# A hybrid decoder block on one core: new places in SBUF for the operands and weights of the split-precision matmuls

## The chip, the cores and the metric

The kernel runs on one core of one Trainium2 chip. The metric is the device time of one execution in microseconds, lower is better; the kernel before takes 1353.78 us (median of 3 runs, 1351.4 to 1355.38).

## The reference, cut to what matters

One layer of a decoder trunk is applied to a prompt of 256 tokens and to 8 sequences of 4 new tokens with state. All of it is float32; the model width is 2048.

```python
mod = silu(c) @ w_ada + b_ada                       # six parts of 2048: shift, scale, gate, twice
h = rmsnorm(x, norm1) * (1 + sc1) + sh1
proj = h @ w_in                                     # pooled channels, z, x/B/C, dt: 4632 columns
pool_out, new_pool = pool_mixer(u_pool, ...)        # windows 2, 4, 8, 16
ssd_out, new_conv, new_ssm = ssd_mixer(z, xbc, dt_raw, ...)   # conv, chunked scan, 24 heads
x = x + g1 * (concat(pool_out, ssd_out) @ w_out)
h2 = rmsnorm(x, norm2) * (1 + sc2) + sh2
up = h2 @ w_up                                      # gate and value, 2 x 5504 columns
x = x + g2 * ((silu(conv3(gate)) * val) @ w_down)
y = rmsnorm(x, norm_f)
```

The outputs are `y` for both kinds of token and the new pooling, convolution, scan and feed-forward states.

## The kernel before, in words

Features lie on the 128 partitions and the 288 tokens (256 + 32) along the free axis, so each of the four large projections (`w_in`, `w_out`, `w_up`, `w_down`) is a series of matmuls with a 128x128 block of weights as the stationary operand and a 128x288 block of activations streaming past it.

To keep float32 accuracy, both sides are split in two float32r parts, hi (the value rounded) and lo (what is left). `mm3` (lines 257 to 261) then issues three matmuls into one PSUM tile: weights hi x operand hi (line 259), weights hi x operand lo (line 260), weights lo x operand hi (line 261). Each of them loads its own stationary operand, so the hi weights are loaded twice. These triples are most of the kernel: k runs over the 16 blocks of the input width (15 or 14 for the three groups of the down projection), m over the output blocks.

Weights come in as one stream of 512 KB tiles of 1024 columns (`load`, line 229; issued by SyncE) into the buffers `raw`. ScalarE rounds a raw tile into the hi part and VectorE subtracts to give the lo part (`split`, lines 234 to 243) of a buffer `wsp`, 2112 columns (8448 bytes) per partition: hi at column 0, lo at column 1056. A wsp tile holds 8 blocks of weights, 512 bytes each. The class `_W` deals out buffers of `raw` and `wsp` in turn from the pools that are open: pool w1 (RAW1 raw and SPLIT1 split buffers) throughout, w0 (RAW0, SPLIT0) until the last of the six column groups of the input projection, w2 (RAW2, SPLIT2) from the sixth tile of the output projection on. With the values before that is 15 raw buffers, then 10, then 11.

The operand of a projection is 16 tiles `xop` (called h1k, mixk and h2k by stage; `new_operand`, line 194), each [128, 2, 288], 2304 bytes per partition: hi, then lo 1152 bytes on. The operand of the down projection is 17 rotating tiles `ahl` of the same form, made in `up_pair` (line 1143). The tag `xop` also holds the tiles `xf` of the final norm at the end.

`shift` (line 187) puts an unused gap in a pool so that what follows lies at a wanted place; the tuple PHASE gives its sizes in bytes for pools kp, ff, w2 and w0.

The order on the engines comes from a scheduler that keeps the program's priorities; `tc.high_priority` moves the splits ahead and `kpo` pins a few instructions in program order. Beside the projections TensorE runs the adaLN products (`ada_group_units`, `ada_part_units`; lines 339 and 380), which read raw tiles directly, the scan (`ssd_group`), the dt projection (lines 967 and 968, 64 columns of weights with hi and lo side by side in one wsp tile) and, during the gated MLP, the update of the sampled states (`state_units`, line 1181).

Of the kernel before, what the change touches and what calls it, by code (L numbers as in the profile page):

```python
# [11 lines left out]
F32 = mybir.dt.float32  # L12
F32R = mybir.dt.float32r
AF = mybir.ActivationFunctionType
ALU = mybir.AluOpType
PSUM = bass.MemoryType.PSUM

P = 128
D = 2048
KT = D // P  # L20
# [3 lines left out]
N = NP + NS  # L24
# [11 lines left out]
ET = XT + len(UEARLY) + 3 * ZEARLY  # L36
EPS = 1e-6
WU = (14, 2, 6)
RAW1, RAW2 = 10, 1
RAW0, SPLIT0 = 5, 1  # L40
SPLIT1, SPLIT2 = 2, 2
PHASE = (128, 32, 0, 128)
# [17 lines left out]
FK = 3  # L60
DGROUPS = [(0, 15), (15, 14), (29, 14)]
RAWC = 1024
CW = 3 + NP + NB * 7
CV = CW - 3

# [8 lines left out]
def _xbc_chunks(gi):  # L74
    k0, gk = KGROUPS[gi]
    mper = RAWC // (gk * P)
    return [(list(range(k0, k0 + gk)), list(range(m, min(m + mper, ET)))) for m in range(0, ET, mper)]
# [20 lines left out]
def _stream():  # L98
# [6 lines left out]
    for gi, (k0, gk) in enumerate(KGROUPS):  # L105
        per = RAWC // (256 * gk)
        for q in range(KT // per):
            s.add(("ada", gi, q), RAWC)
        if gi == len(KGROUPS) - 1:
# [5 lines left out]
    for part in (3, 4, 2, 5):  # L115
        for k in range(KT):
            for h in range(2):
                s.add(("adap", part, k, h), RAWC)
    for m in range(16):
# [16 lines left out]
def kernel(ctx: ExitStack, tc, ins, outs):  # L136
    nc = tc.nc
# [3 lines left out]
    kp = ctx.enter_context(tc.tile_pool(name="kp", bufs=1))  # L141
# [42 lines left out]
    xhi = [None]  # L184
    xlo = [None]
# [6 lines left out]
    shift(kp, PHASE[0], "x")  # L192

    def new_operand(name):
        pair = [kp.tile([P, 2, N], F32R, tag="xop", name=f"{name}k{k}", bufs=KT) for k in range(KT)]
        xhi[0] = [t[:, 0, :] for t in pair]
        xlo[0] = [t[:, 1, :] for t in pair]

    def col_sums(ps, src, rhs, first, last):

# [23 lines left out]
    wp = [None]  # L224

    def load(key):
        off, cols = S.items[key]
        t = wp[0].tile([P, RAWC], F32, tag="raw", name="raw_" + "_".join(map(str, key)))
        nc.sync.dma_start(t[:, :cols], wflat[off:off + P * cols].rearrange("(p n) -> p n", p=P))
        return t  # L230

    kpo = tc.keep_in_program_order

    def split(raw, a, n, name, eng=None, pin=False):
        pair = wp[0].tile([P, 2 * RAWC + 64], F32R, tag="wsp", name="wsp_" + name)
        hi, lo = pair[:, 0:RAWC], pair[:, RAWC + 32:2 * RAWC + 32]
        with tc.high_priority():
            i = nc.scalar.copy(hi[:, :n], raw[:, a:a + n])  # L238
            j = (eng or nc.vector).tensor_tensor(lo[:, :n], raw[:, a:a + n], hi[:, :n].bitcast(F32), ALU.subtract)  # L239
        if pin:  # L240
            kpo(i)
            kpo(j)
        return hi, lo

    def split_hi():
        pair = wp[0].tile([P, 2 * RAWC + 64], F32R, tag="wsp", name="wsp_xbc0_0")
        raw = load(("xbc", 0, 0))
        kpo(nc.scalar.copy(pair[:, 0:RAWC], raw))
        return pair, raw

    def split_xbc(gi, ci, pin=False):
        (ks, ms), key = _xbc_chunks(gi)[ci], ("xbc", gi, ci)
        return ready.pop(key, None) or split(load(key), 0, len(ms) * len(ks) * P, f"xbc{gi}_{ci}",
                                             nc.gpsimd if ci in PSPLIT.get(gi, ()) else None, pin)
# [8 lines left out]
    ready = {}  # L263
    first = []
# [134 lines left out]
    def samp(ap):  # L399
        return ap.rearrange("p (b l) -> p b l", b=NB)  # L400
# [20 lines left out]
    def normalize(k0, gk, r):  # L421
        xv = xav(k0, gk)
        kpo(nc.vector.tensor_tensor(xv, xv, r.unsqueeze(1).to_broadcast([P, gk, N]), ALU.mult))
# [58 lines left out]
    for q in range(4):  # L482
        t = mx.tile([P, 4, N], F32, tag="blk", name=f"xa{q}", bufs=4)
# [26 lines left out]

    cvp = [mx.tile([P, 5, CW], F32, tag="cvp", name=f"cvp{g}", bufs=4) for g in range(4)]

# [141 lines left out]
    def drain(gen):  # L654
        for _ in gen:
            pass
# [3 lines left out]
    def conv_group(g):  # L660
        cf = m2[0].tile([P, 5, CW], F32, tag="cf", name=f"cf{g}", bufs=2)
        cfs[g] = cf
# [46 lines left out]
    def ssd_group(g):  # L709
# [3 lines left out]
        def toks(r, c):  # L713

            return cff[:, r * CW + c * P:r * CW + c * P + P]

# [192 lines left out]
    shift(w0, PHASE[3], "v")  # L909
    wp[0].add(w0, RAW0, SPLIT0)  # L910
    modulate1(0, 1, "g0")
    pair, raw = first.pop()
    kpo(nc.vector.tensor_tensor(pair[:, RAWC + 32:2 * RAWC + 32], raw, pair[:, 0:RAWC].bitcast(F32), ALU.subtract))
    ready[("xbc", 0, 0)] = pair[:, 0:RAWC], pair[:, RAWC + 32:2 * RAWC + 32]
    ready[("xbc", 0, 1)] = split_xbc(0, 1, True)
    normalize(1, 3, rstd1)
    conv0 = conv_group(0)
# [35 lines left out]
    for gi in range(len(KGROUPS)):  # L953
        last = gi + 1 == len(KGROUPS)
        if last:
            wp[0].remove(w0)
            w0_ctx.close()
            m2[0] = mx_ctx.enter_context(tc.tile_pool(name="m2", bufs=1, reuse_waits="tile"))
            raw = load(("dt",))[:, 0:KT * 32].rearrange("p (k h) -> p k h", h=32)
            both = wp[0].tile([P, 2 * RAWC + 64], F32R, tag="wsp", name="wsp_dt")  # L960
            bv = both[:, 0:KT * 64].rearrange("p (k h) -> p k h", h=64)
            with tc.high_priority():
                nc.scalar.copy(bv[:, :, 0:32], raw)
                nc.vector.tensor_tensor(bv[:, :, 32:64], raw, bv[:, :, 0:32].bitcast(F32), ALU.subtract)
            ps = pm.tile([P, 512], F32, tag="mm", name="mm_dt")
            for k in range(KT):
                nc.tensor.matmul(ps[0:64, :N], bv[:, k, :], xhi[0][k], start=k == 0, stop=False)
                nc.tensor.matmul(ps[0:64, :N], bv[:, k, :], xlo[0][k], start=False, stop=k == KT - 1)
            dt_stage(ps)
        else:  # L970
            if gi == 3:
                nc.sync.dma_start(vec, ins["vec"])
            if gi == 4:
                late_loads()
            nxt = ada_group_units(gi + 1)
            k0, gk = KGROUPS[gi + 1]
        for i, m in enumerate(xbc_units(gi)):
            if not last:
                if gi == 0 and i in (4, 10, 16):
                    normalize(4 + 4 * ((i - 4) // 6), 4, rstd1)  # L980
                if i in VISIT[gi + 1][1]:
                    next(nxt)
                if i == ET - MOD[gi]:
                    drain(nxt)
                    modulate1(k0, gk, f"g{gi + 1}")
            else:
                pull(back, 0.5 if m < 20 else RB1) if m >= 9 else None
                pull(adas, RA1 / AY)
# [34 lines left out]
    for g in range(4):  # L1023
        for t in range(3):
            k = 4 + 3 * g + t
# [7 lines left out]
    ff = ctx.enter_context(tc.tile_pool(name="ff", bufs=1, reuse_waits="tile"))  # L1033
# [85 lines left out]
    def up_pair(j):  # L1119
        pg = up0[2 * j] if j < FK else project(("gate", j), KT)  # L1120
        gb = ff.tile([P, NG], F32, tag="gb", name=f"gb{j}", bufs=2)
        gs = gb[:, 2 + NP:].rearrange("p (b l) -> p b l", b=NB)
        nc.gpsimd.memset(gb[:, 0:2], 0.0)
        nc.gpsimd.tensor_copy(gs[:, :, 0:2], stf[:, j])
        nc.scalar.copy(gb[:, 2:2 + NP], pg[:, 0:NP])
        nc.scalar.copy(gs[:, :, 2:6], samp(pg[:, NP:N]))
        nc.gpsimd.tensor_copy(nff[:, j, 0:2], gb[:, NP:NP + 2])
        nc.gpsimd.tensor_copy(nff[:, j, 2:18].rearrange("p (b l) -> p b l", b=NB), gs[:, :, 4:6])
        fw = V_FW + 3 * j
        gc = ff.tile([P, NG], F32, tag="gc", name=f"gc{j}", bufs=2)  # L1130
        nv = NG - 2
        nc.vector.tensor_scalar(gc[:, :nv], gb[:, 0:nv], vec[:, fw:fw + 1], vec[:, V_FB + j:V_FB + j + 1],
                                ALU.mult, ALU.add)
        for i in (1, 2):
            nc.vector.scalar_tensor_tensor(out=gc[:, :nv], in0=gb[:, i:i + nv], scalar=vec[:, fw + i:fw + i + 1],
                                           in1=gc[:, :nv], op0=ALU.mult, op1=ALU.add)
        nc.scalar.activation(gc[:, :nv], gc[:, :nv], AF.Silu)
        pv = up0[2 * j + 1] if j < FK else project(("val", j), KT)
        act = ff.tile([P, N], F32, tag="act", name=f"act{j}", bufs=2)
        nc.vector.tensor_tensor(act[:, 0:NP], gc[:, 0:NP], pv[:, 0:NP], ALU.mult)  # L1140
        gcs = gc[:, 2 + NP:].rearrange("p (b l) -> p b l", b=NB)[:, :, 0:NL]
        nc.vector.tensor_tensor(samp(act[:, NP:N]), gcs, samp(pv[:, NP:N]), ALU.mult)
        ahl = ff.tile([P, 2, N], F32R, tag="ahl", name=f"ahl{j}", bufs=17)
        ah, al = ahl[:, 0, :], ahl[:, 1, :]
        nc.scalar.copy(ah, act)  # L1145
        nc.vector.tensor_tensor(al, act, ah.bitcast(F32), ALU.subtract)
        acts[j] = (ah, al)
# [232 lines left out]
```

## Time and profile before

| | |
|---|---|
| median of 3 runs | 1353.78 us |
| profiled execution, its own time | 1351.28 us |
| its span | 1349.3 us |
| TensorE busy | 1327.1 us (98%) |
| weight loads busy | 1242.1 us (92%) |
| VectorE, ScalarE, GpSimd busy | 819.4, 580.0, 229.0 us |
| granted TensorE clock | 0.997 mean |
| DMA, mean | 240 GB/s |

The profile is one execution. A group line reads: line of the kernel, engine, operation, tile written <- tiles read, shape, count | busy time in us, mean duration in ns | idle time of the engine before them and what ended it. Matmuls are pipelined, so their durations overlap and their ends are modelled: the distance from start to start is what counts. Where a line gives three durations, they are shortest/median/longest in ns, followed by the first and last start in us. A line that begins with two times joined by a colon is a stretch of the span, with the busy time and the count of each engine in it, the granted clock, the share of DMA time and GB/s.

### The profile page before, as it was taken

To read this page: it belongs to the slowest core of one execution; us is meant where nothing else is said; L and a number is where in the kernel's file an instruction comes from. 1 tells how busy PE (TensorE), PEld (TensorE's weight loads), DVE (VectorE), ACT (ScalarE), POOL (GpSimd) and SP (SyncE) were. 2 spreads that over 40 slices of the span, in tenths; PEclk is the share of its full clock that TensorE was granted. 3 is DMA by queue.
4 is the path that set the end of the run, shared out by engine and by line. 5 is a ranking of instruction groups with operands and counts; after the bars stand their busy time and mean duration, and the time that the engine had idled before them with its cause. 6 is when DMAs were issued, how large, how long until landed. Compare 5 with 4: busy or idle time off the path is not lost.

```text
span 1349.3 us, 26295 instructions
## 1 busy us (share of the span) xinstructions
PE 1327.1 (98%) x10541; PEld 1242.1 (92%) x10541; DVE 819.4 (61%) x1458; ACT 580.0 (43%) x934; POOL 229.0 (17%) x420
## 2 busy tenths in 40 slices
PE   9999999999999999999999999999999999999997
PEld 7889998777779889999999999999999999999997
DVE  5676669878664458655665445656655556666543
ACT  5333344578643335434343333444433334443442
POOL 0201001123222223110221001322210011122221
PEclk9999999999999999999999999999999999999998
DMA  9989779978789777777555565655555655665521
GB/s 379 407 335 360 285 271 336 355 263 333 301 328 368 286 248 253 248 300 246 184 185 184 163 181 184 206 182 198 181 173 165 189 194 188 198 194 187 186 84 70
DMA packets 97193, 323.25 MB, mean 240 GB/s; under 512 B 10736, under 2 KB 19760, under 8 KB 97072
## 3 DMA queue, kind: packets, MB, share of 16 engines
q1 hardware_dynamic: 93168, 310.70, 65.4%
q0 software_dynamic: 3184, 9.69, 1.9%
q8 instruction: 82, 1.34, 0.4%
q10 hardware_dynamic: 720, 1.19, 0.2%
q14 instruction: 39, 0.32, 0.1%
HBM read 309.84 MB, written 10.39 MB: 237 GB/s over the span
## 4 chain that ended last, share of the span: by engine, by line
PE 95%; DVE 2%; ACT 1%; issue 0%; DMA 0%; POOL 0%; DVEq 0%; POOLq 0%; ACTq 0%
PE mm_down L260 7%; PE mm_down L261 7%; PE mm_down L259 7%; PE mm_val L260 6%; PE mm_gate L260 6%; PE mm_gate L259 6%; PE mm_gate L261 6%; PE mm_val L261 6%; PE mm_val L259 6%; PE xbc L259 4%; PE xbc L260 4%; PE xbc L261 4%; PE adap L380 4%; PE mm_out L259 3%; PE mm_out L260 2%; PE mm_out L261 2%
## 5 line engine op out<-in xcount | busy, mean ns | idle before, releaser
L260 PE MATMUL mm_down<-ahl,wsp_down 128*128 128x288 f32 x688 | 204.3, 297 | 0.0
L261 PE MATMUL mm_down<-ahl,wsp_down 128*128 128x288 f32 x688 | 202.8, 295 | 0.0
L259 PE MATMUL mm_down<-ahl,wsp_down 128*128 128x288 f32 x688 | 202.1, 294 | 0.0
L260 PE MATMUL mm_val<-h2k,wsp_val 128*128 128x288 f32 x640 | 190.1, 297 | 0.0
L260 PE MATMUL mm_gate<-h2k,wsp_gate 128*128 128x288 f32 x640 | 190.0, 297 | 0.0
L261 PE MATMUL mm_gate<-h2k,wsp_gate 128*128 128x288 f32 x640 | 188.8, 295 | 0.0
L261 PE MATMUL mm_val<-h2k,wsp_val 128*128 128x288 f32 x640 | 188.8, 295 | 0.0
L259 PE MATMUL mm_gate<-h2k,wsp_gate 128*128 128x288 f32 x640 | 188.8, 295 | 0.0
L259 PE MATMUL mm_val<-h2k,wsp_val 128*128 128x288 f32 x640 | 188.0, 294 | 0.0
L239 DVE TENSOR_TENSOR wsp_down<-raw_down,wsp_down 128x1024 fp32r<-128x1024 f32 x96 | 107.3, 1118 | 121.9 <-ACT wsp_down L238 121.9
L239 DVE TENSOR_TENSOR wsp_gate<-raw_gate,wsp_gate 128x1024 fp32r<-128x1024 f32 x80 | 98.0, 1226 | 133.9 <-ACT wsp_gate L238 132.8
L238 ACT CAST wsp_down<-raw_down 128x1024 fp32r<-128x1024 f32 x96 | 92.2, 960 | 168.0 <-PE mm_down L261 118.2
L238 ACT CAST wsp_gate<-raw_gate 128x1024 fp32r<-128x1024 f32 x80 | 84.0, 1050 | 158.8 <-PE mm_gate L261 75.4
L238 ACT CAST wsp_val<-raw_val 128x1024 fp32r<-128x1024 f32 x80 | 84.1, 1051 | 127.9 <-issue 111.3
L259 PE MATMUL xbc<-h1k,wsp_xbc 128*128 128x288 f32 x448 | 132.5, 301 | 5.1 <-ACT h1k L444 3.1
L260 PE MATMUL xbc<-h1k,wsp_xbc 128*128 128x288 f32 x448 | 132.2, 298 | 0.5 <-DVE h1k L445 0.5
L259 PEld LDWEIGHTS mm_down<-ahl,wsp_down 128*128 128x128 f32 x688 | 129.6, 188 | 0.0
L260 PEld LDWEIGHTS mm_down<-ahl,wsp_down 128*128 128x128 f32 x688 | 129.3, 188 | 0.0
L261 PEld LDWEIGHTS mm_down<-ahl,wsp_down 128*128 128x128 f32 x688 | 129.2, 188 | 0.0
L261 PE MATMUL xbc<-h1k,wsp_xbc 128*128 128x288 f32 x448 | 128.8, 294 | 0.0
L259 PEld LDWEIGHTS mm_gate<-h2k,wsp_gate 128*128 128x128 f32 x640 | 120.5, 188 | 5.0 <-ACT ahl L1145 4.2
L259 PEld LDWEIGHTS mm_val<-h2k,wsp_val 128*128 128x128 f32 x640 | 120.6, 188 | 0.0
(320 smaller groups left out, 2979.5 us busy)
## 6 DMA issues: line engine op xcount, KB each, us to landing
raw_adap<-wflat SPq DMA_DIRECT2D x128, 512.0 KB, 6.7
raw_gate<-wflat SPq DMA_DIRECT2D x80, 512.0 KB, 3.6
raw_val<-wflat SPq DMA_DIRECT2D x80, 512.0 KB, 3.6
raw_ada<-wflat SPq DMA_DIRECT2D x64, 512.0 KB, 9.1
raw_xbc<-wflat SPq DMA_DIRECT2D x55, 512.0 KB, 9.5
raw_down<-wflat SPq DMA_DIRECT2D x48, 512.0 KB, 3.5
raw_out<-wflat SPq DMA_DIRECT2D x32, 512.0 KB, 6.0
raw_down<-wflat SPq DMA_DIRECT2D x32, 384.0 KB, 3.0
```

Of the source, the lines that this page charges most:

```text
L238: i = nc.scalar.copy(hi[:, :n], raw[:, a:a + n])
L239: j = (eng or nc.vector).tensor_tensor(lo[:, :n], raw[:, a:a + n], hi[:, :n].bitcast(F32), ALU.subtract)
L259: nc.tensor.matmul(ps, whi[:, w], bh, start=first, stop=False)
L260: nc.tensor.matmul(ps, whi[:, w], bl, start=False, stop=False)
L261: nc.tensor.matmul(ps, wlo[:, w], bh, start=False, stop=last)
L380: i = nc.tensor.matmul(ps[32 * j:32 * j + 32, :512], sc_c[:, k, :], raw[:, (j % 2) * 512:(j % 2) * 512 + 512], start=(k == ay - 1), stop=( ...
```

## The change

Five things move together. The operand tiles grow from 2304 to 2560 bytes; in them hi begins at byte 16 and lo at byte 1200, 1184 bytes on (4 x 256 + 160), where it was 1152 on. The split weights' tile keeps its size; in it hi begins at byte 16 and lo at byte 4208, 4192 bytes on (16 x 256 + 96), where it was 4224 on. The dt projection's tile begins at byte 16 as well. To make room for the larger tiles (16 xop and 17 ahl, 256 bytes each), RAW1 goes from 10 to 9 and RAW2 from 1 to 0, so there are 14, then 9, then 9 raw buffers. No instruction is added, removed or reordered in the code.

```diff
-RAW1, RAW2 = 10, 1
+RAW1, RAW2 = 9, 0
...
+OPC, WSC = 640, 2 * RAWC + 64
+OPH, OPL = 4, 300
+WH, WL = 4, 1052
...
     def new_operand(name):
-        pair = [kp.tile([P, 2, N], F32R, tag="xop", name=f"{name}k{k}", bufs=KT) for k in range(KT)]
-        xhi[0] = [t[:, 0, :] for t in pair]
-        xlo[0] = [t[:, 1, :] for t in pair]
+        pair = [kp.tile([P, OPC], F32R, tag="xop", name=f"{name}k{k}", bufs=KT) for k in range(KT)]
+        xhi[0] = [t[:, OPH:OPH + N] for t in pair]
+        xlo[0] = [t[:, OPL:OPL + N] for t in pair]
...
     def split(raw, a, n, name, eng=None, pin=False):
-        pair = wp[0].tile([P, 2 * RAWC + 64], F32R, tag="wsp", name="wsp_" + name)
-        hi, lo = pair[:, 0:RAWC], pair[:, RAWC + 32:2 * RAWC + 32]
+        pair = wp[0].tile([P, WSC], F32R, tag="wsp", name="wsp_" + name)
+        hi, lo = pair[:, WH:WH + RAWC], pair[:, WL:WL + RAWC]
...
-            both = wp[0].tile([P, 2 * RAWC + 64], F32R, tag="wsp", name="wsp_dt")
-            bv = both[:, 0:KT * 64].rearrange("p (k h) -> p k h", h=64)
+            both = wp[0].tile([P, WSC], F32R, tag="wsp", name="wsp_dt")
+            bv = both[:, WH:WH + KT * 64].rearrange("p (k h) -> p k h", h=64)
...
-        ahl = ff.tile([P, 2, N], F32R, tag="ahl", name=f"ahl{j}", bufs=17)
-        ah, al = ahl[:, 0, :], ahl[:, 1, :]
+        ahl = ff.tile([P, OPC], F32R, tag="ahl", name=f"ahl{j}", bufs=17)
+        ah, al = ahl[:, OPH:OPH + N], ahl[:, OPL:OPL + N]
```

`split_hi` and the first projection's first tile are rewritten in the same way, with hi and lo handed over as two pieces.

More of the change, by code (lines that the diff above doesn't have):

```diff
@@ L245, in split_hi @@
     def split_hi():
-        pair = wp[0].tile([P, 2 * RAWC + 64], F32R, tag="wsp", name="wsp_xbc0_0")
+        pair = wp[0].tile([P, WSC], F32R, tag="wsp", name="wsp_xbc0_0")
+        hi, lo = pair[:, WH:WH + RAWC], pair[:, WL:WL + RAWC]
         raw = load(("xbc", 0, 0))
-        kpo(nc.scalar.copy(pair[:, 0:RAWC], raw))
-        return pair, raw
+        kpo(nc.scalar.copy(hi, raw))
+        return hi, lo, raw
     def split_xbc(gi, ci, pin=False):
@@ L911 @@
     modulate1(0, 1, "g0")
-    pair, raw = first.pop()
-    kpo(nc.vector.tensor_tensor(pair[:, RAWC + 32:2 * RAWC + 32], raw, pair[:, 0:RAWC].bitcast(F32), ALU.subtract))
-    ready[("xbc", 0, 0)] = pair[:, 0:RAWC], pair[:, RAWC + 32:2 * RAWC + 32]
+    hi, lo, raw = first.pop()
+    kpo(nc.vector.tensor_tensor(lo, raw, hi.bitcast(F32), ALU.subtract))
+    ready[("xbc", 0, 0)] = hi, lo
     ready[("xbc", 0, 1)] = split_xbc(0, 1, True)
```

## Prediction

> **What bounds the kernel now.** I read the page's first part, the granted clock and the chain of waits first.
>
> ```profile
> span 1349.3 us, 26295 instructions
> PE 1327.1 (98%) x10541; PEld 1242.1 (92%) x10541; DVE 819.4 (61%) x1458; ACT 580.0 (43%) x934; POOL 229.0 (17%) x420
> PEclk9999999999999999999999999999999999999998
> PE 95%; DVE 2%; ACT 1%; issue 0%; DMA 0%; POOL 0%; DVEq 0%; POOLq 0%; ACTq 0%
> ```
>
> TensorE is the bound, at full clock, and 95% of the chain is its own work. No other engine can give back more than a few microseconds, so the change is worth what it does to the distance between matmuls. Next, the groups by shape, one line of the three in `mm3` (259 is hi weights x hi operand, 260 hi x lo, 261 lo x hi):
>
> ```profile
> L259 PE MATMUL mm_down<-ahl,wsp_down 128*128 128x288 f32 x688 | 202.1, 294 | 0.0
> L259 PE MATMUL mm_gate<-h2k,wsp_gate 128*128 128x288 f32 x640 | 188.8, 295 | 0.0
> L259 PE MATMUL mm_val<-h2k,wsp_val 128*128 128x288 f32 x640 | 188.0, 294 | 0.0
> L259 PE MATMUL xbc<-h1k,wsp_xbc 128*128 128x288 f32 x448 | 132.5, 301 | 5.1 <-ACT h1k L444 3.1 <-DVE ada L369 1.6 <-ACT cvp L649 0.2
> L259 PE MATMUL mm_out<-mixk,wsp_out 128*128 128x288 f32 x256 | 75.7, 296 | 0.0
> L259 PE MATMUL mm_uz<-h1k,wsp_uz 128*128 128x288 f32 x128 | 40.0, 313 | 0.0
> L259 PE MATMUL mm_up<-h2k,wsp_upk 128*128 128x288 f32 x96 | 27.7, 294 | 1.4 <-ACT h2k L417 1.4
> ```
>
> 688+640+640+448+256+128+96 = 2896 triples. One nanosecond per triple is 2.9 us of the kernel. Durations overlap, so I took the distance from counts and first and last starts, in two stretches that hold nothing but the down projection (720 to 800 us, then 1250 to 1330 us):
>
> ```profile
> L259 PE MATMUL mm_down<-ahl,wsp_down x204: 291/293/294, 720.0 to 799.8; 128*128 128x288 f32 x102
> L260 PE MATMUL mm_down<-ahl,wsp_down x205: 297/297/297, 719.7 to 800.0; 128*128 128x288 f32 x103
> L261 PE MATMUL mm_down<-ahl,wsp_down x204: 292/294/295, 719.9 to 799.7; 128*128 128x288 f32 x102
> L259 PE MATMUL mm_down<-ahl,wsp_down x201: 296/296/297, 1249.9 to 1329.9; 128*128 128x288 f32 x101
> L260 PE MATMUL mm_down<-ahl,wsp_down x201: 297/297/297, 1250.0 to 1330.0; 128*128 128x288 f32 x101
> L261 PE MATMUL mm_down<-ahl,wsp_down x201: 297/298/298, 1249.7 to 1329.7; 128*128 128x288 f32 x101
> ```
>
> Same code, same shape, same clock, two locked patterns. First: 203 steps in 79.8 us, a triple in 393.3 ns. Second: 200 steps in 80.0 us, 400.0 ns. The step between them is 6.7 ns. In the second pattern the three durations add to 891 for 400 ns, so a distance is a duration less 163.6: 297 is 133.4, 291 is 127.4. Line 260 stands at 133.4 in both; 259 and 261 are what differ. The patterns alternate:
>
> ```profile
> 640.00:1330.00 690.00, 690.00 (x5221) 690.00 (x5220) 395.88 (x573) 277.39 (x391) 124.77 (x247) 1.00 0.55 177
> 655.00:675.00 20.00, 20.00 (x155) 20.00 (x154) 11.07 (x15) 8.43 (x13) 2.45 (x6) 1.00 0.53 164
> 680.00:700.00 20.00, 20.00 (x152) 20.00 (x151) 11.70 (x17) 7.71 (x12) 5.73 (x9) 1.00 0.57 188
> 705.00:725.00 20.00, 20.00 (x155) 20.00 (x154) 11.68 (x18) 7.02 (x10) 3.98 (x8) 1.00 0.60 188
> 1290.00:1330.00 40.00, 40.00 (x303) 40.00 (x302) 18.85 (x28) 19.75 (x29) 9.05 (x14) 1.00 0.11 34
> ```
>
> 155 matmuls in 20 us, then 152, then 155 (columns: TensorE, weight loads, VectorE, ScalarE, GpSimd, clock, DMA share, GB/s). The slow pattern stays at a DMA share of 0.11 and at 0.57, so traffic is not its cause. What flips it is a pair of other matmuls put in between, the state update's, whose weights `bm` lie in two buffers 1152 bytes (half a raster of 256) apart:
>
> ```profile
> 677.18 0.51 PE L1181 MATMUL hs<-xm,bm 128*128 128x384 f32 x2
> 677.52 0.29 PE L259 MATMUL mm_gate<-h2k,wsp_gate 128*128 128x288 f32 x1
> 703.12 0.51 PE L1181 MATMUL hs<-xm,bm 128*128 128x384 f32 x2
> 703.47 0.29 PE L259 MATMUL mm_gate<-h2k,wsp_gate 128*128 128x288 f32 x1
> ```
>
> After 677 the slow pattern holds, after 703 the fast one. Their PSUM tiles alternate as well, so this points to place without proving it. The mean between 640 and 1330: less 32 such matmuls (16 pairs of 0.34 to 0.35 us, 5.5 us) and 2 that overlap the edges, 684.5 us over 5187 matmuls, 132.0 each, 395.9 a triple: 39% of the way from fast to slow. With the 1167 triples of the first 640 us at 393.3, the mean is 394.9.
>
> **The change, part by part.** (1) No instruction is added or removed; addresses move. Now all tiles are multiples of 256 bytes (2304, 4096, 8448), so every first part sits at one place of a 256-byte raster, and both second parts (1152 = 4.5 x 256, 4224 = 16.5 x 256) half a raster on. After, first parts are 16 bytes further, the operand's second part 160 and the weights' 96 bytes beyond them. While 259 and 261 stream, the weights loaded for the next matmul still lie at the operand's own place; while 260 streams, they lie 64 bytes behind it, where today they are level. So 260's distance and the turns from hi to lo are what change.
>
> Does place bear on distance at all? The trace has no run with these offsets; the nearest rows are matmuls with other relations of place:
>
> ```profile
> L968 PE MATMUL mm_dt<-h1k,wsp_dt x16: 292/294/299, 190.3 to 194.2; 128*64 128x288 f32 x16
> L968 PEld LDWEIGHTS mm_dt<-h1k,wsp_dt x16: 134/134/138, 190.2 to 194.1; 128*64 128x64 f32 x16
> L1181 PE MATMUL hs<-xm,bm x32: 331/336/338, 677.2 to 1245.7; 128*128 128x384 f32 x32
> ```
>
> Identical instructions differ by 7 ns, the same step again. Line 968 loads half the columns (134 against 188 ns) and is no closer, 128.4 to 135.4, so the length of the load isn't the limit; what remains is how starts fall. The bounds of a distance from rows are 127.4 (291) and 135.4 (299): a triple between 382 and 406, that is (382-394.9) x 2.896 = -37 us to (406-394.9) x 2.896 = +32 us. A gain isn't excluded, since 260 is never seen below 133.4 where its neighbours reach 127.4; a loss isn't either, since 968 streams a lo operand and reaches 135.4. I take one step down, 260 from 133.4 to 126.7, as 260 is the one whose relation is altered and both neighbours show the lower place: -6.7 x 2.896 = -19.3 us, with the mix of patterns kept.
>
> The Trainium skill, "SBUF — State Buffer", section "Who interferes with whom", speaks against this: TensorE has two independent SBUF read ports and never waits on anyone, so place would be worth 0. The same skill's "TensorE: Matmul & The Clock Gate" ("Wait — 56ns, not 53.3ns?") gives 288/2.4 + 2.5 = 122.5 ns as an estimate; the trace has 131 to 133, and by that figure the kernel would stand 79 us lower whatever the places. The trace's excess and its two patterns agree with neither.
>
> (2) One raw buffer fewer: 15 to 14 until the input projection's last group, 10 to 9 until the output projection's sixth tile, then 11 to 9. Rows:
>
> ```profile
> SPq L229 <- DVE wsp_down L239: 204.8, 82, 3.9
> SPq L229 <- PE adap L380: 87.1, 35, 9.0
> raw_out<-wflat SPq DMA_DIRECT2D x32, 512.0 KB, 6.0
> raw_gate<-wflat SPq DMA_DIRECT2D x80, 512.0 KB, 3.6
> ACT wsp_xbc L238 <- DMA raw_xbc<-wflat: 14.4, 3, 5.4
> ```
>
> SyncE waits for free buffers, so loads run as far ahead as buffers allow. In the gate, value and down stages a half tile feeds 24 matmuls (24 x 132 = 3.2 us); nine buffers are 28 us ahead of a landing of 3.6 us: free. In the output stage landing takes 6.0 us with adaLN loads in between, still less than nine loads ahead. Only three waits on a weight landing exist at the start, 14.4 us of ScalarE time. I take +1 us; bounds 0 and +6 (each wait later by one landing's spacing, about 2 us).
>
> (3) Splits: 16 bytes off could slow ScalarE and VectorE.
>
> ```profile
> L238 ACT CAST wsp_val<-raw_val 128x1024 fp32r<-128x1024 f32 x80 | 84.1, 1051 | 127.9 <-issue 111.3 <-PE mm_down L261 7.2 <-PE mm_val L261 5.7
> L239 DVE TENSOR_TENSOR wsp_val<-raw_val,wsp_val 128x1024 fp32r<-128x1024 f32 x80 | 99.9, 1249 | 32.8 <-ACT wsp_val L238 31.6
> ```
>
> 1051 + 1249 = 2300 ns stand against 3.2 us of matmuls per half tile, with four split buffers: 0. Both would have to take 40% longer before a half tile waits; with no cover at all a half tile would cost those 2.3 us.
>
> Sum against the profiled execution, 1351.3 us (span 1349.3 and 2.0 around it): -19.3 + 1 = 1333.0. The median shown is 2.5 above that execution: **1335.5 us**.
>
> **Rivals.**
> *A, two steps a triple* (386.7 becomes 380): every matmul at the shortest distance seen. -38.6 + 1: 1316. For: 259 does reach 127.4. Against: never all three, and quantised starts let one gain be taken back in the next turn.
> *B, place is worth nothing*, the change doesn't do what it says; this is the ports' rule taken at its word. Only the pattern mix shifts: all fast is -1.6 x 2.896 = -4.6, unchanged 0; with +1 us 1350 to 1355. Against: the flips at the state update.
> *C, the slow pattern everywhere*: with the lo parts off the half raster, the triple locks at 400.0 as from 1250 us on. (400-394.9) x 2.896 = +14.8 and +1: 1369.6. For: it is stable for 80 us without a break, and line 968 shows a lo operand at 135.4 when its weights aren't level with it. It decides from the point where slow triples exceed today's mix, 39% after 640 us.
> *D, buffers*: no gain in distance, and the start and the turn to the gated MLP starve, +6 to +15: 1360 to 1369. Against: 95% TensorE in the chain.
>
> **How the numbers follow.** Forecast 0.42, A 0.14, B 0.17, C 0.19, D 0.08. The forecast's own range is 1330 (fast pattern throughout, no buffer cost) to 1341 (+6 for buffers). The range to hold 8 in 10 reaches into A and toward C: 1312 to 1364. A change of 0.3% (4 us) is about what a measurement can tell: below 1349.7 lie the forecast, A and a third of B, 0.61; within it the rest of B, 0.13; above it C and D, 0.26.
>
> **What would show it.** In the changed kernel's down stretches, count triples: 386.7 ns means 207 in 80 us, against 203 and 200 now. Line 260's median duration should fall from 297 to about 290 with 259 and 261 where they are. If 260 falls but 259 or 261 rises by 7, the step was given back and B holds. If all stand at 296 to 298, C. If distances are right but the total isn't, look for ScalarE waits on raw landings before 110 us and at 495 us: D. Wrong altogether would be a change of distance that isn't near a multiple of 6.7 ns, or one in the projections with tiles `xop` but not in those with `ahl`, as both get the same offsets.

## The result, and the profile after

The changed kernel takes 1367.26 us (median of 4 runs, 1365.89 to 1368.53), the kernel before 1354.58 us beside it (4 runs, 1351.4 to 1355.84). The ratio is 1.0097, with a 95% interval of 1.0075 to 1.0119: slower, by about 1%. I had forecast 1335.5 us and the other sign. What happened is rival C, for which I had put 1369.6 us and a chance of 0.19.

In the changed kernel the three lines of `mm3` are 263, 264 and 265, where they were 259, 260 and 261; the splits are 241 and 242, the state update is 1185. From its profile's page, the span, the engines' busy time and the chain that ended last:

```profile
span 1363.9 us, 26255 instructions
PE 1341.8 (98%) x10541; PEld 1254.9 (92%) x10541; DVE 820.8 (60%) x1458; ACT 579.9 (43%) x934; POOL 234.1 (17%) x420
PE 94%; DVE 3%; ACT 2%; issue 1%; DMA 1%; POOL 0%; DVEq 0%; ACTq 0%; POOLq 0%
```

As many matmuls as before (10541) are busy for 14.7 us longer, and the span is 14.6 us longer (1363.9 against 1349.3, one profiled execution of each). The engine that bounds the kernel is the one that lost. The three lines by shape, and the same stretch of the down projection as in the prediction:

```profile
L263 PE MATMUL mm_down<-ahl,wsp_down 128*128 128x288 f32 x688 | 203.7, 296 | 0.0
L264 PE MATMUL mm_down<-ahl,wsp_down 128*128 128x288 f32 x688 | 203.0, 295 | 0.0
L265 PE MATMUL mm_down<-ahl,wsp_down 128*128 128x288 f32 x688 | 202.9, 295 | 0.0
...
L263 PE MATMUL mm_down<-ahl,wsp_down x189: 296/296/296, 724.5 to 799.6; 128*128 128x288 f32 x189
L264 PE MATMUL mm_down<-ahl,wsp_down x189: 295/295/295, 724.6 to 799.8; 128*128 128x288 f32 x189
L265 PE MATMUL mm_down<-ahl,wsp_down x189: 295/295/295, 724.7 to 799.9; 128*128 128x288 f32 x189
```

188 steps in 75.2 us are 400.0 ns a triple, and every one of them is alike: shortest, median and longest duration agree. Before, this stretch ran at 393.3. The 400.0 isn't the slow pattern of before over again. From start to next start, the three lines take 133, 134 and 133 ns here; before, they take 134, 134 and 132 in the slow pattern and 128.7, 133.3 and 131.3 in the fast one. The stretches of the changed kernel (columns as in the prediction: busy time and count of TensorE, weight loads, VectorE, ScalarE, GpSimd, then clock, DMA share and GB/s):

```profile
655.00:675.00 20.00, 20.00 (x152) 20.00 (x152) 13.74 (x18) 8.16 (x13) 7.25 (x12) 1.00 0.57 180
705.00:725.00 20.00, 20.00 (x152) 20.00 (x151) 12.50 (x19) 8.26 (x14) 4.89 (x11) 1.00 0.61 191
640.00:1330.00 690.00, 690.00 (x5169) 690.00 (x5168) 395.40 (x574) 273.96 (x386) 123.55 (x247) 1.00 0.57 180
```

The two stretches that held 155 matmuls now hold 152, as the slow one between them always did. Between 640 and 1330 us there are 5169 matmuls instead of 5221; with the prediction's own working (684.5 us over 5135) that is 133.3 each, 399.9 a triple.

From the starts of all undisturbed triples in the two traces, the mean went from 395.2 to 399.7 ns. With 2896 triples that is +13.0 us. Taken over all matmuls of `mm3`, with each distance cut at 150 ns, the distances add to 1147.7 us before and 1160.1 after (+12.4); what longer gaps behind these lines have beyond the 150 ns is 22.9 and 24.6 us (+1.7). The rest of the 14.6 us is 0.5.

### The profile page after: what moved, and what is told of

It reads as the page before. It is cut to its first block, busy times and chain, and to the rows that moved or that the text cites. A ratio compares the mean times of both kernels' runs of the same rounds, so it can differ in the third digit from the quotient of the medians.

```text
span 1363.9 us, 26255 instructions
## 1 busy us (share of the span) xinstructions
PE 1341.8 (98%) x10541; PEld 1254.9 (92%) x10541; DVE 820.8 (60%) x1458; ACT 579.9 (43%) x934; POOL 234.1 (17%) x420
## 4 chain that ended last, share of the span: by engine, by line
PE 94%; DVE 3%; ACT 2%; issue 1%; DMA 1%; POOL 0%; DVEq 0%; ACTq 0%; POOLq 0%
PE mm_down L265 7%; PE mm_down L263 7%; PE mm_down L264 7%; PE mm_gate L263 6%; PE mm_val L265 6%; PE mm_gate L265 6%; PE mm_val L263 6%; PE mm_gate L264 6%; PE mm_val L264 6%; PE xbc L263 4%; PE xbc L264 4%; PE xbc L265 4%; PE adap L384 4%; PE mm_out L263 3%; PE mm_out L265 3%; PE mm_out L264 2%
## 5 line engine op out<-in xcount | busy, mean ns | idle before, releaser
L242 DVE TENSOR_TENSOR wsp_val<-raw_val,wsp_val 128x1024 fp32r<-128x1024 f32 x80 | 100.3, 1253 | 34.2 <-ACT wsp_val L241 32.1
```

## The experiments

All kernels but the three maps are the changed kernel with other values of five constants, in floats: OPC, the length of an operand tile; OPH and OPL, where its hi and lo begin; WH and WL, where hi and lo of the weights begin. A setting is four places in the 256-byte raster: hi and lo of the operand, hi and lo of the weights. The tiles themselves begin at byte 224 of it. All these kernels have the changed kernel's smaller set of raw buffers (14, then 9, then 9). The theories that the expectations set against each other were, in words: the buffers or the larger tiles cost the time; the 16 bytes do; the operand's second part does; the weights' second part does; or none does alone, and the places act together.

**Buffers and tile size.** First the places of before with the smaller set of raw buffers, then those places in tiles of 2560 bytes.

```diff
-OPC, WSC = 640, 2 * RAWC + 64        # e1_buffers
+OPC, WSC = 576, 2 * RAWC + 64
-OPH, OPL = 4, 300                    # e1_buffers and e2_tile
-WH, WL = 4, 1052
+OPH, OPL = 0, 288
+WH, WL = 0, 1056
```

> Old places throughout (operand tiles of 2304 bytes, lo half a raster on, no 16 bytes), but one raw buffer fewer as in the changed kernel. Theory C1 (the second parts' places lock the triples at 400.0 ns): the mix of before comes back, triples of 393.3 with 400.0 between some state updates, 203 to 204 triples in 80 us of the down projection, a span of 1350 to 1353 us. Theory C2 (the 16 bytes do it): the same. Theory C3 (tiles of 2560 bytes do it): the same. Theory D (the buffers do it): triples as before but stalls, span near 1360 to 1364.

> Operand tiles of 2560 bytes, everything else at the old places (no 16 bytes, lo half a raster on, one raw buffer fewer). C1 and C2: the mix of before, span 1350 to 1354. C3 (with 2560 all tiles have one place modulo 512 where 2304 alternates): 400.0 everywhere, span 1362 to 1366.

Measured, with one execution of each: 1353.64 and 1357.03 us, against 1354.88 for the kernel before on the same chip. Executions of the kernel before range from 1351.25 to 1357.23 us in this record, so these single times decide nothing, and the counts have to. The long stretch, first with fewer buffers:

```profile
640.00:1330.00 690.00, 690.00 (x5222) 690.00 (x5221) 397.19 (x578) 277.81 (x390) 124.71 (x247) 1.00 0.57 179
```

and with the larger tiles as well:

```profile
640.00:1330.00 690.00, 690.00 (x5221) 690.00 (x5220) 398.44 (x581) 276.92 (x389) 121.43 (x249) 1.00 0.57 179
```

5222 and 5221 matmuls, as before (5221), and the same mix of 393.3 and 400.0 ns; the mean triple is 395.25 and 395.26. Neither edit touches the distances. The gaps behind `mm3` rise by 3.3 and 3.5 us in these profiles. So the loss in the distances comes from the places.

**One part of the places at a time.** Everything 16 bytes on; then the two second parts alone.

```diff
-OPH, OPL = 4, 300
-WH, WL = 4, 1052
+OPH, OPL = 4, 292                    # e3_shift16
+WH, WL = 4, 1060
+OPH, OPL = 0, 296                    # e4_lo
+WH, WL = 0, 1048
```

> First parts 16 bytes further, second parts still half a raster beyond them (operand 1152, weights 4224), tiles of 2560 bytes. C1: the mix of before, span 1350 to 1354, since nothing moves against anything else but the state update and adaLN matmuls. C2: 400.0 everywhere, span 1362 to 1366.

> First parts at their old place, second parts 1184 (operand) and 4192 bytes (weights) on as in the changed kernel, tiles of 2560 bytes. C1: 400.0 everywhere, span 1362 to 1366. C2: the mix of before, 1350 to 1354. If both e3 and e4 show the old mix, only the two together lock it.

Measured, again with one execution of each: 1354.28 and 1355.39 us, against 1354.88. The long stretch with the 16 bytes alone:

```profile
640.00:1330.00 690.00, 690.00 (x5246) 690.00 (x5245) 400.14 (x582) 279.40 (x393) 122.85 (x251) 1.00 0.58 180
```

and with the second parts alone:

```profile
640.00:1330.00 690.00, 690.00 (x5225) 690.00 (x5224) 398.34 (x580) 278.21 (x392) 122.21 (x249) 1.00 0.57 179
```

Neither contains a stretch at 400.0. The 16 bytes give 393.3 in some stretches (132, 131, 130 ns, the same in every triple) and 395.6 in others, 394.4 in the mean. The second parts give 395.6 nearly throughout, in a pattern that repeats only after three triples (401, 395 and 391 ns). Added up against 395.2, the parts should leave the changed kernel at 394.7; it stands at 399.7.

**Two parts at a time.** The 16 bytes with the operand's second part, and with the weights'.

```diff
-OPH, OPL = 4, 300
-WH, WL = 4, 1052
+OPH, OPL = 4, 300                    # e5_oplo
+WH, WL = 4, 1060
+OPH, OPL = 4, 292                    # e6_wlo
+WH, WL = 4, 1052
```

> As the changed kernel, but the weights' second part back at half a raster (4224 bytes on): 16 bytes, operand lo 160 on. Neither half of the change locked 400.0 by itself (394.4 and 395.5 ns a triple). Theory E1 (the operand's lo together with the 16 bytes lock it): 399.7 a triple, span near 1364. Theory E2 (the weights' lo with the 16 bytes lock it): 393 to 396, span 1350 to 1354. Theory E3 (all three are needed): 393 to 396 here and in the next run.

> As the changed kernel, but the operand's second part back at half a raster (1152 bytes on): 16 bytes, weights' lo 96 on. E1: 393 to 396 ns a triple, span 1350 to 1354. E2: 399.7, span near 1364. E3: 393 to 396.

Measured, one execution of each: 1357.43 and 1351.68 us, against 1352.78. The mean triples are 396.5 and 394.6 ns; no stretch at 400.0 in either. Of the combinations run, only all three places together hold the triples at 400.0: every theory that gave the loss to one part, or to the 16 bytes with one second part, has fallen.

**The triples alone.** A kernel that runs nothing but `mm3`: 16 triples into one tile, for 128 settings (hi at byte 224 or 240 of the raster, for operand and weights alike; each second part 0 to 224 bytes on, in steps of 32), each entered behind a matmul of 100 and then of 180 columns. Hi at 224 is the place of before, 240 that of the change.

> Leaves out the whole computation but for the matmuls' form: nothing but triples on operands and weights that lie in SBUF from the start, 128 settings of the places (first parts at byte 224 or 240 of the 256-byte raster; the operand's lo 0, 32, ... 224 beyond it modulo 256, the weights' lo likewise), two stretches of 16 triples each, and before each stretch one matmul of 100 or 180 columns so that it starts at another point. Theory of locks (the triple's time is set by these four places alone): the settings of the kernels so far give their times again, 393.3 or 400.0 for before, 400.0 for the changed one, 393.3 or 395.6 for 16 bytes alone, 395.6 for the lo parts alone, and nothing lies off 360 to 410. Theory that the other engines' traffic has a part in it: distances here differ from those, near one value for all settings. If any setting is under 390 in both stretches, it makes a kernel that beats both.

With DMA, VectorE, ScalarE and GpSimd all but idle the triples take 386.7 to 402.9 ns (the very first series of the run, at 412.6, left out). Three settings of it, 13 triples each; those of before (224, 128 on, 128 on), of the change (240, 160, 96) and the fastest of the map (240, 128, 64). The first and last starts give 393.3, 400.0 and 386.7 ns:

```profile
L170 PE MATMUL mm<-op,ws x13: 297/297/297, 481.9 to 486.6; 128*128 128x288 f32 x13
L171 PE MATMUL mm<-op,ws x13: 292/292/295, 482.0 to 486.7; 128*128 128x288 f32 x13
L169 PE MATMUL mm<-op,ws x13: 291/291/294, 482.2 to 486.9; 128*128 128x288 f32 x13
...
L170 PE MATMUL mm<-op,ws x13: 295/295/296, 1397.1 to 1401.9; 128*128 128x288 f32 x13
L171 PE MATMUL mm<-op,ws x13: 295/295/295, 1397.3 to 1402.1; 128*128 128x288 f32 x13
L169 PE MATMUL mm<-op,ws x13: 296/296/296, 1397.4 to 1402.2; 128*128 128x288 f32 x13
...
L170 PE MATMUL mm<-op,ws x13: 289/289/289, 1281.7 to 1286.4; 128*128 128x288 f32 x13
L171 PE MATMUL mm<-op,ws x13: 294/294/294, 1281.9 to 1286.5; 128*128 128x288 f32 x13
L169 PE MATMUL mm<-op,ws x13: 288/288/288, 1282.0 to 1286.6; 128*128 128x288 f32 x13
```

Lines 169, 170 and 171 are hi x hi, hi x lo and lo x hi. The durations are those of the whole kernels: 291, 297, 292 to 294 before, 296, 295, 295 after. The partial settings come out as in the kernels too (from the starts, for the two entries): 395.6 and 395.6 for the 16 bytes alone, 395.5 twice for the second parts alone, 396.7 twice for the operand's with the 16 bytes, 393.3 and 395.0 for the weights' with them. So the places of these four streams are enough for the difference between 393.3 and 400.0, with memory traffic and the other engines all but idle (VectorE is busy for 7% of the span). One thing the map doesn't show: the 400.0 that the kernel before takes in part of its stretches came from neither entry here.

**The fastest setting of the map, in the kernel.**

```diff
-OPH, OPL = 4, 300
-WH, WL = 4, 1052
+OPH, OPL = 4, 292                    # e7_w64
+WH, WL = 4, 1044
```

> The changed kernel with two numbers altered: the operand's lo back at half a raster (1152 bytes on), the weights' lo 64 bytes on modulo 256 (4160) in place of 96; first parts 16 bytes on, one raw buffer fewer. In the map of places this setting alone gave 386.7 ns a triple, from both starts. Theory of locks: 386.7 through the stretches that hold matmuls alone, 207 triples in 80 us of the down projection; (386.7 - 395.2) x 2896 triples = -25 us against before and +1 to +3 for the buffers as in e1: span 1327 to 1331, time 1328 to 1334. If the surroundings (state update, adaLN, traffic) throw it into another lock, 393 to 400 and 1350 to 1366.

Measured: 1350.36 us (1346.89 to 1354.68) against 1354.03; ratio 0.998, 0.9966 to 0.9993. That is about a seventh of the gain expected. First the kernel before in the stretch from 375 to 625 us:

```profile
375.00:625.00 250.00, 246.95 (x1887) 223.33 (x1879) 140.93 (x235) 101.02 (x158) 47.99 (x94) 1.00 0.80 291
```

and this one there and later, with the four adaLN transposes (line 304) behind which its triples change:

```profile
375.00:625.00 250.00, 248.53 (x1907) 222.74 (x1908) 142.05 (x238) 100.11 (x155) 49.17 (x93) 0.99 0.81 289
640.00:1330.00 690.00, 690.00 (x5232) 690.00 (x5231) 394.26 (x571) 277.51 (x391) 123.26 (x249) 1.00 0.56 178
...
636.67 0.60 PE L304 MATMUL adat_p<-early,asb_p 128*128 128x128 f32 x4
637.03 0.38 PE L263 MATMUL mm_gate<-h2k,wsp_gate 128*128 128x288 f32 x1
```

From 375 to 625 us the triples take 386.7 ns in every long series but one (395.1, from 480 to 491 us), and that stretch holds 1907 matmuls instead of 1887. Before 375 us the two times take turns. From the transposes at 637 us to the end the triples take 395.0 (684.5 us over 5198 matmuls: 131.7 each), and none of the 16 state updates brings 386.7 back; the mean triple of the whole kernel is 393.0. The same places have two times, and the kernel fell from one into the other. The transposes at this point change the pattern in the kernel before too, there from 400.0 to 393.3.

**A wider map**: 250 settings in steps of 16 bytes, operand and weights apart.

> A second map of the same form as the first, and like it without the computation: 250 settings in which all four places vary in steps of 16 bytes (operand's hi and weights' hi apart too), among them before, the changed kernel, the 386.7 setting and its neighbours, the rest drawn at random. Theory of locks: before 393.3 or 400.0, changed 400.0, the third 386.7 as in the first map; other values again few and repeated. If the relation of one pair alone (operand's lo to its hi, say) set the time, settings with the same value of it would agree; by the first map they don't, and 386.7 should vanish with any 16-byte step in any of the four. Settings at 386.7 or below are expected in about 1 of 100.

Without the first series of the run, the range is 386.7 to 406.7 ns, and the commonest times are 400.0 and 393.3. Before and changed come out as expected, the third setting doesn't: where the first map had 386.7 from both entries, both take 395.0 here over whole repeats of their pattern (400, 398, 394 and 388 ns), though the entries are the same two matmuls of 100 and 180 columns. So the length of the matmul ahead doesn't by itself fix which time is taken. The lowest, 386.7, came from both entries for three settings of the 250: hi at 112 and at 144 with second parts 128 and 64 on, which were tried next, and operand's hi at 64 with lo 208 on, weights' hi at 16 with lo 32 on, which was not tried in the kernel. Another setting, operand's hi at 48 with lo at the same place of the raster (1280 bytes on), weights' hi at 192 with lo 16 bytes on, gave 390.0 from both.

One family in this map is moved through the raster as a whole, in 16 steps of 16 bytes: hi of both at the same place, second parts 128 and 64 on. With hi at an odd multiple of 16 the triples take 386.7 or 395.0; with hi at an even multiple they take 398.3, from both entries each time. For this family a shift by 32 bytes leaves the times that occur as they are, and a shift by 16 doesn't.

**Two other settings at 386.7.**

```diff
-OPH, OPL = 4, 300
-WH, WL = 4, 1052
+OPH, OPL = 36, 324                   # e8_hi112
+WH, WL = 36, 1076
+OPH, OPL = 44, 332                   # e9_hi144
+WH, WL = 44, 1084
```

> The same distances between the parts as in the run with the weights' lo 64 on (operand lo 1152, weights lo 4160 bytes on), but both first parts at byte 144 of their tiles, that is byte 112 of the 256-byte raster in place of 240. In the second map this place gave 386.6 ns from both starts, where 240 gave 386.7 in one map and 395.6 in the other, as that kernel did: 386.7 up to 635 us, 395 after. Theory of several stable locks (place sets which there are, the history which one is taken): with 112, 386.7 in nearly all stretches, among them the down projection (207 triples in 80 us), span 1326 to 1333. If the surroundings alone decide, 393 to 396 after 640 us as before, span 1343 to 1350.

> As the run with 112, but first parts at byte 144 of the raster (byte 176 of their tiles). In the second map 386.6 from both starts as well. Several stable locks: as there, span 1326 to 1333. If only one of the two keeps 386.7, the map's two starts weren't enough to show which places have a second lock; surroundings alone: 1343 to 1350.

Measured: 1350.68 us (ratio 0.998, 0.9967 to 0.9993) and 1346.0 us (0.9947, 0.993 to 0.9963), against 1353.07. Both miss by far more than their intervals. In the first, 386.7 is there before 637 us, as with the earlier setting, and 395.0 from there to the end. Three stretches of the second, and the two state updates at which it changes over:

```profile
640.00:700.00 60.00, 60.00 (x457) 60.00 (x457) 36.59 (x50) 24.96 (x38) 14.08 (x27) 1.00 0.59 190
705.00:810.00 105.00, 105.00 (x817) 105.00 (x816) 53.79 (x75) 37.05 (x41) 7.32 (x22) 1.00 0.58 180
830.00:1330.00 500.00, 500.00 (x3791) 500.00 (x3791) 287.73 (x422) 205.43 (x299) 98.69 (x191) 1.00 0.56 176
...
701.00 0.52 PE L1185 MATMUL hs<-xm,bm 128*128 128x384 f32 x2
701.36 0.29 PE L263 MATMUL mm_gate<-h2k,wsp_gate 128*128 128x288 f32 x1
...
818.91 0.51 PE L1185 MATMUL hs<-xm,bm 128*128 128x384 f32 x2
819.26 0.29 PE L263 MATMUL mm_gate<-h2k,wsp_gate 128*128 128x288 f32 x1
```

Between the two updates a matmul takes 128.5 ns (105 us over 817), 386.7 a triple by the starts; ahead of them and behind them 131 to 132, 395.0 a triple. An update breaks the series for 0.35 us, and the series that starts again may settle otherwise.

**How often each time is taken.** Triples alone again: 14 settings, each entered behind a matmul of 12 different lengths (40 to 276 columns); then 32 settings in which hi and lo lie at one place each, and both kernels' places with 256, 272 and 320 columns.

> Leaves out the computation like the two maps. Part A: 14 settings of the places, those of before, of the changed kernel and of the runs with 16 bytes, lo parts and so on among them, each entered from 12 different starts (one matmul of 40 to 276 columns ahead). Theory of several stable locks: before comes out at 393.3 from some starts and at 400.0 from others, the changed kernel at 400.0 from all 12, the lo parts alone at 395.6 from all, 16 bytes alone at 393.3 or 395.6, the three kernels with the weights' lo 64 on at 386.7 or 395.0. Rival, one lock to a setting with a slow approach: all 12 starts agree for each setting, and what differs in the kernels comes from their surroundings. Part B: no lo parts at all, one place for the operand and one for the weights, 16 differences between them at byte 224 and 240. If streams and loads disturb each other by their difference alone, the two bytes give the same row of values; a triple of 3 x 122.5 to 3 x 136 is the whole room. Part C: before and changed with 256, 272 and 320 columns in place of 288: if the lock is a matter of where streams end in the raster, 256 and 320 (whole and quarter rasters) shift the times by other amounts than 32 columns' worth, 40 ns a triple by the rate of 120 ns for 288.

The places of the change, from the first length and from a later one:

```profile
L169 PE MATMUL mm<-op,ws x13: 289/289/289, 94.7 to 99.3; 128*128 128x288 f32 x13
L170 PE MATMUL mm<-op,ws x13: 292/292/292, 94.8 to 99.5; 128*128 128x288 f32 x13
L168 PE MATMUL mm<-op,ws x13: 292/292/292, 94.9 to 99.6; 128*128 128x288 f32 x13
...
L169 PE MATMUL mm<-op,ws x13: 295/295/295, 139.9 to 144.7; 128*128 128x288 f32 x13
L170 PE MATMUL mm<-op,ws x13: 295/295/295, 140.1 to 144.9; 128*128 128x288 f32 x13
L168 PE MATMUL mm<-op,ws x13: 296/296/296, 140.2 to 145.0; 128*128 128x288 f32 x13
```

Same instructions and places, 386.7 ns in the first series and 400.0 in the second (12 steps in 4.64 and 4.80 us by the unrounded starts). Counted over the 12 entries, with the time over whole repeats once the series has settled, for nine of the 14 settings:

| places | triple, ns (entries) |
|---|---|
| before | 393.3 (11); the first series of the run is left out |
| changed | 400.0 (11), 386.7 (1) |
| 16 bytes alone | 395.6 (11), 393.3 (1) |
| second parts alone | 395.6 (12) |
| those of e7_w64, e8_hi112, e9_hi144 | 386.7 (5, 6, 5), else 395.0 |
| operand's hi at 64, lo 208 on; weights' hi at 16, lo 32 on | 386.7 (8), 400.0 (4) |
| operand's hi at 48, lo 0 on; weights' hi at 192, lo 16 on | 390.0 (12) |

Two of the expectations failed: the places of before gave no 400.0 from any entry, and those of the change gave 386.7 from one. So what throws the kernel before into its 400.0 isn't among these entries. The rival of one time to a setting, approached slowly, falls: five of the settings in the table settle at two times 8 to 13 ns apart. The last row is the lowest time that came from every entry. In the second part of this kernel, settings with the same difference between operand and weights but begun at 224 or at 240 don't agree (difference 48: 393.3 against 400.0; 144: 390.0 or 393.3 against 404.0), so the time isn't a function of the difference alone. In the third, 256 columns take 353.3 ns at the places of before and 351.3 to 353.4 at those of the change, 272 columns 373.3 to 374.8 and 366.7 or 376.7, 320 columns 440.0 at both: the same places that lose at 288 columns lose nothing at 256 and 320, and at 272 they win in three entries of four.

**The setting with a single time, in the kernel.**

```diff
-OPH, OPL = 4, 300
-WH, WL = 4, 1052
+OPH, OPL = 20, 340                   # e10_one
+WH, WL = 56, 1084
```

> Other places with the same tiles: operand's hi at byte 48 of the 256-byte raster and its lo 1280 bytes on, weights' hi at byte 192 and their lo 4112 on; one raw buffer fewer as in all of these. In the maps this setting gave 390.0 ns a triple from all 12 starts, and from the two of the second map. Theory that places set the stable times and history chooses among them: with only one to choose, the kernel holds 390.0 from the projections to the end whatever comes between, state update and adaLN included: 205 triples in 80 us of the down projection, (390.0 - 395.2) x 2896 = -15 us and +1 to +3 for buffers, span 1335 to 1339, ratio 0.990 to 0.993. Rival, the surroundings (traffic, other engines, the places of the other matmuls) set the time and the maps only show what holds without them: 393 to 400 in parts of the kernel, a span above 1343.

Measured: 1343.68 us (1340.83 to 1343.83) against 1354.24; ratio 0.9915, 0.99 to 0.993. That ratio is the one expected; the span, 1342.1, is 3 us above the span expected. Its first 110 us, a late stretch, and the down projection:

```profile
0.00:110.00 110.00, 101.54 (x1016) 88.81 (x1017) 69.12 (x195) 43.79 (x93) 8.67 (x8) 0.97 0.90 347
640.00:1310.00 670.00, 670.00 (x5144) 670.00 (x5143) 390.75 (x570) 271.89 (x383) 122.07 (x243) 1.00 0.59 184
...
L263 PE MATMUL mm_down<-ahl,wsp_down x206: 294/295/296, 719.7 to 799.7; 128*128 128x288 f32 x103
L264 PE MATMUL mm_down<-ahl,wsp_down x206: 288/290/291, 719.9 to 799.8; 128*128 128x288 f32 x103
L265 PE MATMUL mm_down<-ahl,wsp_down x206: 289/291/293, 720.0 to 800.0; 128*128 128x288 f32 x103
```

205 steps in 80.0 us are 390.2 ns, and the late stretch gives 390.1 with all the state updates in it (5144 less 34, in 664.5 us). No update knocked it out: behind each the triples come back to 390.0 within the series. The distances add to 1135.2 us, 12.5 below before, and the longer gaps to 27.0, 4.1 above. Part of the time lost is at the start: the first 110 us, at a mean clock of 0.97, hold 1016 matmuls, where the changed kernel has 1040 at a clock of 1.00:

```profile
0.00:110.00 110.00, 102.69 (x1040) 89.91 (x1041) 70.99 (x200) 44.78 (x94) 8.68 (x8) 1.00 0.92 358
```

A lower clock in that stretch isn't peculiar to these places: it is 0.98 in the profile of e1_buffers too, with the places of before and 1033 matmuls. Four of the five executions of this version had a mean clock of 0.993 and spans of 1341.5 to 1342.1 us; the fifth, at 0.996, took 1339.1. What lowers the clock wasn't tried. This version is faster than both kernels: by 0.85% than before, and by the two ratios (0.9915 / 1.0097) 1.8% than the changed one.

## Why the prediction was wrong, point by point

**What bounds the kernel: right.** TensorE had 95% of the chain and has 94%; the change was worth what it did to the distance between matmuls, 12.4 of the 14.6 us.

**The step that failed** is in part (1): "I take one step down, 260 from 133.4 to 126.7, as 260 is the one whose relation is altered and both neighbours show the lower place". It takes a triple for a sum of three distances, each with a place of its own on the scale, of which one can be moved while the others stay. The runs show something else. The three matmuls keep one rhythm together. Each setting of the four places has one or a few stable times for the whole triple, or for two, three or four triples, and which of them is taken depends on what went before the series. Line 260 didn't lose a step: in the changed kernel line 264 stands at 134 ns, and 263 and 265, which I had left where they were, both went to 133. The term was put at -19.3 us and measured +12.4 to +13.0. The parts don't add up either: with 16 bytes alone, second parts alone, and the 16 bytes with one second part, the mean triple lies between 394.4 and 396.5, and with all together at 399.7.

The reading under that step was off as well. I took distances from durations, whose ends are modelled. By the starts, 260 and 261 differ between the two patterns by 0.7 ns each and 259 by 5.3, so it is 259 that differs, hardly 261; and 261 takes 130 to 132 ns in the fast pattern, so only one neighbour, 259 with 127 to 130, comes near the lower place of 126.7.

**The step of 6.7 ns: right, as far as it went.** 386.7, 393.3, 400.0 and 440.0 are 58, 59, 60 and 66 such steps; but 395.0 and 395.6 are 59.25 and 59.33 of them, in patterns that repeat after four and three triples, and 390.0 is 58.5, though in 8 of its 12 entries every triple takes 390 ns alike.

**The bounds, 382 to 406: nearly right.** The stable times in the maps run from 386.7 to 406.7. The bounds were taken per matmul, and single distances from 125 to 144 ns occur in the maps, outside the 127.4 to 135.4 that I had from rows.

**The flips at the state update: the rows were read rightly, the reason was too narrow.** I pointed to the buffers of `bm`. In the maps there is no `bm`, and behind nothing but another matmul and the series ahead of it the same places take 386.7 or 395.0 (those of e7_w64), or 386.7 or 400.0 (the change's). Other breaks do it as well, as the transposes at 637 us did. In the kernel before, the updates lead into 400.0 and back to 393.3 by turns; why was not taken apart further.

**The ports' rule.** By the Trainium skill, "SBUF — State Buffer", section "Who interferes with whom", which the prediction had weighed as rival B, place would have cost nothing. The map of triples disagrees: with every other engine all but idle, places alone move a triple of one shape from 386.7 to over 400 ns. What in the chip does it, no run here can show. The 122.5 ns a matmul that the prediction estimated by the Trainium skill's "TensorE: Matmul & The Clock Gate" ("Wait — 56ns, not 53.3ns?") were not reached: the lowest stable time found, 386.7 a triple, is 128.9 each.

**The buffers, taken at +1 with bounds 0 and +6: right.** With the smaller set of raw buffers alone the gaps behind `mm3` rose by 3.3 us in the profile, and in the changed kernel by 1.7, both within the bounds; the run's time was 1.2 us below its neighbour's, one execution of each. **The splits, taken at 0: right**; the two engines' busy time moved by 1.4 and 0.1 us.

**Rival C was the outcome, and its size was about right, in part by luck**: +14.8 us for the triples and +1 for the buffers, against +13.0 (395.2 to 399.7 ns) and +1.7, and 14.6 in the span. The 400.0 was taken over from the slow pattern of before; nothing in the working said that the new places would settle at just that time, where the parts of the change settle at 393.3, 395.0, 395.6 or 396.7. Its argument, that the slow pattern had held without a break for 80 us, was the best evidence in the trace, since it showed a rhythm that keeps itself up. Its condition was wrong: "with the lo parts off the half raster" alone the triples stand at 395.5. I gave it 0.19, because I took the slow pattern for a mishap of the kernel before, to be weighed by how often it occurs there (39% after 640 us), and not as one of several states, any of which new places may have as theirs. The sums over the chances are a little off too: C and D make 0.27, not 0.26, and no part of B's 1350 to 1355 us lies below 1349.7.

**What stays open**: which resource makes four byte offsets set the rhythm, and which entry leads into which time. The difference of places alone doesn't set it; that one family keeps its times under shifts by 32 bytes and not by 16 is a hint that wasn't followed up. The prediction's line 968 spoke already against the length of the weight load. I can list the stable times of a setting by running it, and can't derive them.

## What to carry to other kernels

Where matmuls follow each other without a gap, read the distance over whole repeats of the pattern, and don't price an edit by moving one line's distance with the others held. Try new places in a small kernel that runs the series alone, entered from a dozen different starts, and choose the setting whose slowest stable time is lowest, not the one with the lowest time: 390.0 from every start gave 0.85%, 386.7 from about half the starts gave 0.2 to 0.5%. Two starts were too few here: the same two gave 386.7 in one map and 395.0 in the next. Repeat it for each number of columns, since the places that lose at 288 don't at 320.

## What the runs showed of the hardware that was not expected

At one shape and at full clock, a triple of float32r matmuls took from 386.7 to 406.7 ns by places alone, 5%. The same places and the same instructions took 386.7 ns from one start and 400.0 from eleven others, and kept that time until something else was put in between. A shift of all parts by 16 bytes, with every difference between them unchanged, took away the 400.0 of the kernel before and put 395.6 in its place. In the one family that was moved through the raster in steps of 16 bytes, the eight even steps gave 398.3 and the eight odd ones 386.7 or 395.0.
